# Gate and up projections of a streaming encoder layer by one level of Strassen's products

## Chip, core and metric

The kernel runs on one core of one Trainium2 chip. The metric is the device time of one execution in microseconds (us), median of three runs.

## What is computed

One layer of a hybrid encoder for 1024 prompt tokens and 32 sample tokens, width 1024: a combined projection, sparse attention, retention, a gated merge, and at the end the part that the change touches:

```
x1 = layer_norm(ALPHA * x + merged @ w_o, ln1_g, ln1_b)
h = jax.nn.silu(x1 @ w_gate) * (x1 @ w_up)          # w_gate, w_up: 1024 x 2816
return layer_norm(ALPHA * x1 + h @ w_down, ln2_g, ln2_b)   # w_down: 2816 x 1024
```

All inputs and outputs are float32.

## The kernel before

TensorE works on pairs of rounded numbers: every operand is split into a high part (`hi`, written as type `fp32r` by ScalarE) and a remainder (`lo = x - hi`, by VectorE or GpSimd), and each product is made of three matmuls, hi·hi, hi·lo and lo·hi, accumulated in PSUM (`tform` and `natural`, whose matmuls are all recorded by `chain`, L163). `split` (L139, L143) makes a pair; `unit` loads a 128x1024 weight tile into `raw` (two buffers), and splits it into `whi`, `wlo` (four buffers in `ring1`).

The tokens are 1056 columns: nine tiles of 128 (the last, tile 8, holds the 32 sample tokens), in three chunks of 384, 384 and 288 columns. A program on the host, `Weave`, sets the order of TensorE's instructions; the other engines' instructions are put in order by a scheduler, and each engine then works through its own in that order.

The end of the layer has two stages. `o_jobs` multiplies by w_o, tile by tile, in two halves of 512 columns. In the second half a layer norm follows each tile, and `x1_tile` transposes the result on TensorE (L988) and splits it into x1, eight tiles of 128 rows. `f_jobs` then goes through the 22 blocks of 128 hidden columns: for each chunk, 24 matmuls for gate (8 tiles of k, three products each), SiLU on ScalarE (L1085), 24 matmuls for up, a multiplication on VectorE out of PSUM (L1087), and the split of the result into `hh`, `hl`. After each second block, `down` adds the previous pair's part of h @ w_down: per token tile two outputs of 512 columns, 6 matmuls each, which VectorE adds to `yn` (L1058). The last call takes two pairs at once and ends each tile with the second layer norm.

PSUM has two banks under the name `g` and six under `m`; `f_jobs` uses the `m` ones.

Of the kernel before, what the change touches and what calls it, by code (L numbers as in the profile page):

```python
# [21 lines left out]
FB = 22  # L22
ALPHA = 2.0 ** 0.25
# [72 lines left out]
def body(ctx, tc, nc, a):  # L96
# [120 lines left out]
    mt_d = [dp.tile([D, n], F32, name=f"mtd{j}") for j, (_, n) in enumerate(CHUNKS)]  # L217
    r_d, r32_d = scratch(1, [8, 1152], "rd")[0], scratch(1, [8, 32, 1152], "r32")[0]
# [18 lines left out]
    def mbank():  # L237
        return psum.tile([128, 512], F32, name="m", bufs=6)
# [741 lines left out]
    def x1_tile(t, t_ln):  # L980
        c0, n = SEGS[t]
        j, o0 = chunk_of(t)
        yield 0.0, t_ln
        for q in range(2):
            pt = mbank()
            for i in range(4):
                k = q * 4 + i
                nc.tensor.transpose(pt[:, i * n:(i + 1) * n], yn[t][0:n, k * 128:(k + 1) * 128], ident[0:n, 0:n])  # L988
            split(x1[j][0][:, q * 4:(q + 1) * 4, o0:o0 + n], x1[j][1][:, q * 4:(q + 1) * 4, o0:o0 + n],
                  pt[:, 0:4 * n].rearrange("p (k c) -> p k c", k=4), "act", "dve")  # L990
# [40 lines left out]
    mtp.close()  # L1031
    ringE = Open("ringE", bufs=2, side="right")
    hp = Open("hid", side="right")
    g2 = hp.tile([128, D], F32, name="g2")
    b2 = hp.tile([128, D], F32, name="b2")
    dma(g2, bcast(a["ln2_g"], D))
    dma(b2, bcast(a["ln2_b"], D))

    def down(pairs, final):
        us = [u for pr in pairs for u in pr[0]]  # L1040
        for t in (8, *range(8)) if final else range(9):
            c0, n = SEGS[t]
            for hf in range(2):
                kk = [(u[0][:, hf * 512:(hf + 1) * 512], u[1][:, hf * 512:(hf + 1) * 512]) for u in us]
                o = mbank()
                if t < 8:
                    yield from natural(o, kk, lambda k: (pairs[k // 2][1][:, k % 2, c0:c0 + n],
                                                         pairs[k // 2][2][:, k % 2, c0:c0 + n]), 512)
                    src = o
                else:  # L1050
                    yield from natural_s(o, kk, lambda k: pairs[k // 2][3][:, k % 2, :], 512, hp)
                    src = merge_s(o, 512, hp)
                y = yn[t][0:n, hf * 512:(hf + 1) * 512]
                if final:
# [7 lines left out]
    def f_jobs():  # L1062
        def load(f):
            return blk(unit(a["w_gate"][f], ring1)), blk(unit(a["w_up"][f], ring1))

        prev = None
        nxt = load(0)
        for f in range(FB):
            i = f % 2
            if i == 0:  # L1070
                hh = hp.tile([128, 2, TT], F32R, name="hh", bufs=2)
                hl = hp.tile([128, 2, TT], F32R, name="hl", bufs=2)
                hs = hp.tile([128, 2, 64], F32R, name="hs", bufs=2)
            wg, wu = nxt
            if f + 1 < FB:
                nxt = load(f + 1)
            else:
                wl = [unit(a["w_down"][f - 1 + z], ring1) for z in range(2)]
            for j, (c0, n) in enumerate(CHUNKS):
                def rx(k):  # L1080
                    return x1[j][0][:, k, :], x1[j][1][:, k, :]
                pg, pu = mbank(), mbank()
                yield from tform(pg, wg, KT, rx, n)
                sg = hp.tile([128, 384], F32, name="sg", bufs=2)
                nc.scalar.activation(sg[:, :n], pg[:, :n], AF.Silu)  # L1085
                yield from tform(pu, wu, KT, rx, n)
                nc.vector.tensor_tensor(sg[:, :n], pu[:, :n], sg[:, :n], op=ALU.mult)  # L1087
                split(hh[:, i, c0:c0 + n], hl[:, i, c0:c0 + n], sg[:, :n], "act", "dve")
                if c0 + n == TT:
                    for jj, tl in enumerate((hh, hl)):  # L1090
                        nc.scalar.activation(hs[:, i, jj * 32:(jj + 1) * 32], f32(tl[:, i, T:TT]), AF.Copy)
            if i == 1:
                if f + 1 < FB:
                    if prev is not None:
                        yield from down([prev], False)
                    prev = ([unit(a["w_down"][f - 1 + z], ringE) for z in range(2)], hh, hl, hs)
        yield from down([prev, (wl, hh, hl, hs)], True)
# [128 lines left out]
```

## Time and profile before

| | |
|---|---|
| median of three runs (lowest to highest) | 1974.81 us (1972.91 to 1975.71) |
| the profiled execution | 1969.68 us, span 1967.6 us |
| TensorE matmul busy | 1918.1 us, 97% of the span |
| VectorE, ScalarE, GpSimd busy | 1141.0, 644.4, 654.2 us |
| gate, up and down stage | from about 1175 us of the span to its end |

Busy time of TensorE is a model of pipelined matmuls; how fast it goes is read from the distance between the starts of matmuls. A wait of another engine matters only where TensorE waits for that engine.

### The profile page before, as it was taken

What the parts mean: (1) busy time and instruction counts of PE and PEld (TensorE: products, weight loads), DVE (VectorE), ACT (ScalarE), POOL (GpSimd) and SP (SyncE); (2) the same over time, 40 slices, a digit from 0 to 9 for tenths busy, and PEclk for the clock granted to TensorE, in tenths of its full rate; (3) what the DMA queues carried; (4) which work ended last, traced back from release to release, by engine and by line L of the source; (5) the groups of instructions that cost most, each with busy time, mean ns of one, the idle gap of its engine ahead of it and who ended that gap; (6) DMA issues with size and microseconds to landing.
All of it is one profiled execution on the core that took longest, in us unless ns stands there. A gap on an engine that the chain in (4) does not pass through costs nothing. (4 is left out here: it accounts for less than half of the span.)

```text
span 1967.6 us, 28831 instructions
## 1 busy us (share of the span) xinstructions
PE 1918.1 (97%) x10785; PEld 1745.3 (89%) x10785; DVE 1141.0 (58%) x2335; ACT 644.4 (33%) x1352; POOL 654.2 (33%) x631
## 2 busy tenths in 40 slices
PE   8999999999999799999999999999999999999998
PEld 7899898787788799899999779998998998999896
DVE  4699889999981687876533483233333233324327
ACT  4553322423332555555422353121121121122122
POOL 4464443545454344442222233131132032032021
PEclk9999999999999899999999999999999999999999
DMA  5255642313217656534646532110110121011012
GB/s 182 86 171 202 223 134 80 94 50 92 57 53 190 176 151 163 149 113 138 222 131 198 163 105 79 40 65 16 50 65 33 33 65 44 22 65 54 12 42 89
DMA packets 138068, 201.40 MB, mean 102 GB/s; under 512 B 18992, under 2 KB 107048, under 8 KB 137928
## 3 DMA queue, kind: packets, MB, share of 16 engines
q1 hardware_dynamic: 131016, 190.90, 31.9%
q10 hardware_dynamic: 6912, 8.65, 1.3%
q8 instruction: 85, 1.39, 0.3%
q14 instruction: 55, 0.45, 0.1%
HBM read 149.06 MB, written 51.62 MB: 102 GB/s over the span
## 5 line engine op out<-in xcount | busy, mean ns | idle before, releaser
L143 POOL TENSOR_TENSOR wlo<-raw,whi 128x1024 fp32r<-128x1024 f32 (+1 forms) x132 | 319.3, 2424 | 820.8 <-ACT whi L139 770.3
L163 PE MATMUL m<-x,whi 128*128 128x384 f32 (+1 forms) x2112 | 504.4, 324 | 0.0
L163 PEld LDWEIGHTS m<-x,whi 128*128 128x128 f32 x2112 | 371.8, 189 | 1.4
L163 PE MATMUL m<-x,wlo 128*128 128x384 f32 (+1 forms) x1056 | 343.4, 325 | 0.0
L1087 DVE TENSOR_TENSOR sg<-m,sg 128x384 f32<-128x384 f32 (+1 forms) x66 | 34.6, 524 | 321.0 <-PE m L163 320.3
L139 ACT ACTIVATE whi<-raw 128x1024 fp32r<-128x1024 f32 x140 | 146.5, 1057 | 191.6 <-PE m L163 57.2
L163 PE MATMUL g<-xh,whi 128*128 128x384 f32 (+1 forms) x600 | 198.5, 331 | 0.5 <-ACT gev L673 0.5
L163 PE MATMUL g<-xh,wlo 128*128 128x384 f32 (+1 forms) x600 | 198.5, 331 | 0.2 <-POOL wlo L143 0.2
L163 PEld LDWEIGHTS m<-x,wlo 128*128 128x128 f32 x1056 | 198.5, 188 | 0.0
L163 PE MATMUL g<-xl,whi 128*128 128x384 f32 (+1 forms) x600 | 198.1, 330 | 0.0
L360 DVE MAX8 m<-sc 128x8 f32<-128x384 f32 (+6 forms) x209 | 182.3, 875 | 4.7
L361 DVE MATCH_REPLACE8 sc<-m,sc 128x384 f32<-128x384 f32 (+6 forms) x209 | 179.9, 861 | 0.2
L1058 DVE TENSOR_TENSOR yn<-m,yn 128x512 f32<-128x512 f32 x144 | 99.5, 691 | 94.6 <-PE m L163 94.6
L163 PE MATMUL m<-whi,hh 128*128 128x512 f32 x352 | 139.1, 395 | 0.0
L163 PE MATMUL m<-whi,hl 128*128 128x512 f32 x352 | 138.9, 395 | 0.0
L163 PE MATMUL m<-wlo,hh 128*128 128x512 f32 x352 | 138.5, 393 | 0.0
L744 POOL TENSOR_TENSOR P<-TB,mask 128x128 f32<-128x128 f32 (+8 forms) x72 | 92.7, 1304 | 126.2 <-PE m L806 98.1
L163 PEld LDWEIGHTS g<-xh,whi 128*128 128x128 f32 x600 | 113.4, 189 | 3.6 <-ACT gev L673 0.8
L163 PEld LDWEIGHTS g<-xl,whi 128*128 128x128 f32 x600 | 113.4, 189 | 2.8 <-issue 1.1
L163 PEld LDWEIGHTS g<-xh,wlo 128*128 128x128 f32 x600 | 113.7, 189 | 2.4 <-POOL wlo L143 0.5
L143 DVE TENSOR_TENSOR hl<-sg,hh 128x384 fp32r<-128x384 f32 (+1 forms) x66 | 75.6, 1146 | 53.0 <-ACT hh L139 53.0
L163 PE MATMUL g<-whi,xl 128*128 128x512 f32 x256 | 105.4, 412 | 0.0
(243 smaller groups left out, 3866.5 us busy)
## 6 DMA issues: line engine op xcount, KB each, us to landing
raw<-wT SPq DMA_DIRECT2D x34, 512.0 KB, 3.7
raw<-w_gate SPq DMA_DIRECT2D x22, 512.0 KB, 3.2
raw<-w_up SPq DMA_DIRECT2D x22, 512.0 KB, 3.2
raw<-w_down SPq DMA_DIRECT2D x22, 512.0 KB, 3.3
raw<-wr SPq DMA_DIRECT2D x16, 512.0 KB, 3.9
ml<-mtd SPq DMA_DIRECT2D x16, 512.0 KB, 5.8
KS<-kh SPq DMA_DIRECT2D x16, 392.0 KB, 6.4
KL<-kl SPq DMA_DIRECT2D x16, 392.0 KB, 9.1
```

Of the source, the lines that this page charges most:

```text
L139: nc.scalar.activation(hi, src, AF.Copy)
L143: e.tensor_tensor(lo, src, f32(hi), op=ALU.subtract)
L163: nc.tensor.matmul(out, lhsT=l, rhs=r, start=i == 0, stop=i == m - 1)
L360: nc.vector.max(m8[0:n], v)
L361: nc.vector.match_replace(v, m8[0:n], v, TAKEN)
L744: nc.gpsimd.tensor_tensor(pp[0:n, :Wd], TB[0:n, b0:b0 + Wd], masks[t][0:n, :], op=ALU.add)
L1058: nc.vector.tensor_tensor(y, src, y, op=ALU.add)
L1087: nc.vector.tensor_tensor(sg[:, :n], pu[:, :n], sg[:, :n], op=ALU.mult)
```

## The change

Blocks 0 and 1 are computed as before, but in column pieces of 264 (`u_plain`). For the other 20, x1 is kept as four quadrants (two halves of k by two halves of the columns; tile t goes to the half t mod 2, and each half holds 16 of the sample columns twice, so it is 528 wide), and two neighbouring blocks of a weight matrix with their two halves of k are the four quadrants of the other factor. Seven products replace the eight of the plain multiplication (`products`): sums of quadrants of x1 (`sums`: T1, T2, T3 and T4) are made once, T4 in the place of x1's quadrant B12, and sums of the quadrants of the weights for each pair of blocks and matrix (`Quad`) on GpSimd. Each product is 12 matmuls of 264 columns (4 tiles of k, three products), done for both pieces u = 0, 1 of the columns. `products` accumulates further products onto a bank whose earlier content was read out, so some products come after a read-out (`e1`, `u2`, `u3`). h goes to DRAM (`hd_d`), as does the scaled x1 (`x1_d`); `d_jobs` reads h back and does all of down afterwards. In the second half of `o_jobs` tile 8 comes first.

```diff
+HALF, SUB = 528, 264
...
+def place(t):
+    return t % 2, t // 4 * SUB + t // 2 % 2 * 128
...
+    hd_d, x1_d = scratch(FB, [128, 1024], "hd"), scratch(1, [TT, D], "x1d")[0]
...
-    x1 = [[fp.tile([128, KT, n], F32R, name=f"x1{i}_{j}") for i in range(2)] for j, (_, n) in enumerate(CHUNKS)]
+    x1 = [[[fp.tile([128, 4, HALF], F32R, name=f"x1{i}_{q}{h}") for i in range(2)] for h in range(2)] for q in range(2)]
...
     def x1_tile(t, t_ln):
...
+        dma(x1_d[c0:c0 + n, :], yn[t][0:n, :])
...
     def o_jobs():
...
-            for t in range(9):
+            for t in range(9) if hf == 0 else (8, *range(8)):
...
+    def went():
+        i = n_went[0] % 6
+        n_went[0] += 1
+        if i < 4:
+            return [ring1.tile([128, 1024], F32R, name=nm) for nm in ("whi", "wlo")]
+        return [mtp.tile([128, 8, 128], F32R, name=nm).rearrange("p a b -> p (a b)") for nm in ("mh", "ml")]
...
+    def sums(tp, t4):
...
+            whole(a_, B11)
+            whole(b_, B12)
+            nc.vector.tensor_tensor(a_, b_, a_, op=ALU.subtract)
+            whole(c_, B22)
+            nc.vector.tensor_tensor(b_, c_, b_, op=ALU.subtract)
+            nc.vector.tensor_tensor(c_, c_, a_, op=ALU.subtract)
+            cut(tq[2], c_)
+            cut(tq[3], b_)
+            cut(tq[1], a_)
+            whole(b_, B21)
+            nc.vector.tensor_tensor(c_, b_, c_, op=ALU.subtract)
...
+    def u_plain():
+        ws = [(went_of(a["w_gate"][f]), went_of(a["w_up"][f])) for f in range(2)]
+        sg = hg.tile([128, 2, TT], F32, name="sg", bufs=2)
+        while len(W.sides) > 2:
+            yield 0.2
+        for u in range(2):
+            if u == 1:
+                while W.sides:
+                    yield 0.2
+                ynp.close()
+                st["tset"] = Open("tset")
+                for z in range(1, 4):
+                    tq[z] = [st["tset"].tile([128, 4, HALF], F32R, name=f"T{z}{i}") for i in range(2)]
+                tp = Open("tsum", side="right")
+                t4 = tp.tile([128, 4, HALF], F32, name="t4")
+                sums(tp, t4)
+            s = slice(u * SUB, (u + 1) * SUB)
+            for f in range(2):
+                wg, wu = (blk(w) for w in ws[f])
+                for h in range(2):
+                    d = sg[:, f, h * HALF + u * SUB:h * HALF + (u + 1) * SUB]
+
+                    def rx(k):
+                        b = x1[k // 4][h]
+                        return b[0][:, k % 4, s], b[1][:, k % 4, s]
+                    pg, pu = mbank(), mbank()
+                    yield from tform(pg, wg, KT, rx, SUB)
+                    nc.scalar.activation(d, pg[:, :SUB], AF.Silu)
+                    yield from tform(pu, wu, KT, rx, SUB)
+                    nc.vector.tensor_tensor(d, pu[:, :SUB], d, op=ALU.mult)
+        for i in range(4):
+            split(T4[0][:, i, :], T4[1][:, i, :], t4[:, i, :], "act", "dve")
+        store_h(sg, 0)
+        tp.close()
+
+    class Quad:
+        def __init__(self, src, fp_):
+            self.r = [load_raw(src[2 * fp_ + i]) for i in range(2)]
+            a11, a12, a21, a22 = (r[:, z * 512:(z + 1) * 512] for r in self.r for z in range(2))
+            self.s1, self.s2 = (up.tile([128, 512], F32, name=f"qs{z}") for z in range(2))
+            P = nc.gpsimd.tensor_tensor
+            P(self.s1, a21, a22, op=ALU.add)
+            P(self.s2, self.s1, a11, op=ALU.subtract)
+            P(a21, a11, a21, op=ALU.subtract)
+            self.e = [went(), went()]
+            self.put(0, a11, self.s2)
+            self.put(1, a21, self.s1)
+
+        def put(self, i, *srcs):
+            for z, src in enumerate(srcs):
+                c = slice(z * 512, (z + 1) * 512)
+                split(self.e[i][0][:, c], self.e[i][1][:, c], src, "act", "dve")
+
+        def more(self):
+            a12, a22 = (r[:, 512:1024] for r in self.r)
+            self.e.append(went())
+            self.put(2, a12, a22)
+            nc.gpsimd.tensor_tensor(a12, a12, self.s2, op=ALU.subtract)
+
+        def last(self):
+            self.e.append(went())
+            self.put(3, self.r[0][:, 512:1024])
+
+    def products(q, u, sg, gate, hooks, order=range(7)):
+        s = slice(u * SUB, (u + 1) * SUB)
+        pa, pb, pc, pd = gbank(), mbank(), mbank(), mbank()
+        e1, u2, u3 = (up.tile([128, SUB], F32, name=nm, bufs=2) for nm in ("e1", "u2", "u3"))
+        d = [[sg[:, f, h * HALF + u * SUB:h * HALF + (u + 1) * SUB] for h in range(2)] for f in range(2)]
+        add, mul = ALU.add, ALU.mult
+        V, P = nc.vector.tensor_tensor, nc.gpsimd.tensor_tensor
+        todo = ((pa, 0, 0, B11), (pb, 0, 1, tq[2]), (pd, 1, 0, tq[3]), (pc, 1, 1, tq[1]),
+                (pa, 2, 0, B21), (pd, 2, 1, T4), (pc, 3, 0, B22))
+        for z in order:
+            bank, i, c, b = todo[z]
+            w = half_of(q.e[i], c)
+            o = bank[:, :SUB]
+            for k in range(4):
+                for j, (l, r) in enumerate(((0, 0), (0, 1), (1, 0))):
+                    nc.tensor.matmul(o, lhsT=w[l][:, k, :], rhs=b[r][:, k, s], start=z < 4 and k == 0 and j == 0,
+                                     stop=k == 3 and j == 2, skip_group_check=True)
+                    yield mm(SUB)
+            if z == 0:
+                nc.scalar.activation(e1, o, AF.Copy)
+            elif z == 1:
+                V(u2, o, e1, op=add)
+            elif z == 2:
+                V(u3, o, u2, op=add)
+            elif z == 3:
+                V(d[1][1] if gate else u3, o, u3, op=add)
+            elif z == 4:
+                if gate:
+                    nc.scalar.activation(d[0][0], o, AF.Silu)
+                else:
+                    V(d[0][0], o, d[0][0], op=mul)
+            elif z == 5:
+                V(d[1][0] if gate else e1, o, u2, op=add)
+            else:
+                V(d[0][1] if gate else u2, o, u2, op=add)
+            if z in hooks:
+                hooks[z]()
+        for (f, h), t in (((1, 1), u3), ((1, 0), e1), ((0, 1), u2)):
+            if gate:
+                nc.scalar.activation(d[f][h], d[f][h], AF.Silu)
+            else:
+                P(d[f][h], d[f][h], t, op=mul)
...
+    def u_jobs():
...
+        for x, (m, f) in enumerate(seq):
+            q = nxt
+            if m == 0:
+                sg = hg.tile([128, 2, TT], F32, name="sg", bufs=2)
+            if x + 1 < len(seq):
+                nxt = make(*seq[x + 1])
+                hooks = {1: nxt.more, 3: nxt.last}
+            else:
+                first.append(went_of(a["w_down"][0]))
+                first.append(went_of(hd_d[0], "dve"))
+                hooks = {1: lambda: first.append(went_of(a["w_down"][1])),
+                         3: lambda: first.append(went_of(hd_d[1], "dve"))}
+            if x == 0:
+                g = [products(q, u, sg, True, hooks if u else {}, (0, 4, 1, 2, 3, 5, 6)) for u in range(2)]
+                for z in range(2):
+                    for _ in range(24):
+                        yield next(g[z])
+                yield from g[0]
+                yield from g[1]
+            else:
+                yield from products(q, 0, sg, m == 0, {})
+                yield from products(q, 1, sg, m == 0, hooks)
+            if m == 1:
+                store_h(sg, 2 * f)
...
+    def d_jobs():
+        cur = ([0, 1], [first[0], first[2]], [first[1], first[3]])
+        for i in range(FB // 2):
...
+                for z in range(2):
+                    us[z] = went_of(a["w_down"][fs[z]])
+                    hh[z] = h_of(fs[z])
...
+            yield from down(*cur, "first" if i == 0 else "mid")
...
-    def f_jobs():
...
-                if f + 1 < FB:
-                    if prev is not None:
-                        yield from down([prev], False)
...
```

Three places show how the instructions stand. The first is ScalarE where the plain pair ends and the first products begin. Before, the first block of `f_jobs` looks so (`sg<-m` SiLU, `x_2<-m` and `yn` the sample tile's x1, `hh<-sg` and `whi<-raw` splits):

```order
L1085 ACTIVATE sg<-m 128x384
L139 ACTIVATE x_2_12383<-m 128x4x32 x2
L993 ACTIVATE yn_12378<-yn_12378 32x1024
L139 ACTIVATE hh<-sg 128x384
L1085 ACTIVATE sg<-m 128x384
L139 ACTIVATE hh<-sg 128x384
L139 ACTIVATE whi<-raw 128x1024
```

Now, with what each waits for (`x_01<-t` is the high part of T4, `e<-g` the read-out of the first product for u = 0 and, lower, for u = 1; `qs` are the GpSimd sums, `mh<-raw` and `whi<-raw` splits of weight quadrants):

```order
L148 ACTIVATE x_01_12394<-t_13496 128x528 [waits PE_49] x3
L148 ACTIVATE x_01_12394<-t_13496 128x528 [waits DVE_49,PE_49]
L1191 ACTIVATE e_13845<-g 128x264 [waits DVE_49,PE_49]
L1200 ACTIVATE sg<-g 128x264 [waits PE_49]
L148 ACTIVATE mh<-raw 128x512 [waits Pool_49]
L148 ACTIVATE whi<-raw 128x512 [waits Pool_49]
L1191 ACTIVATE e_13877<-g 128x264 [waits PE_49]
```

A read-out that TensorE needs now stands behind a wait for VectorE, and a second one behind splits that wait for GpSimd. The second place is VectorE and GpSimd at the same spot: the end of the sums and the first splits of weights on VectorE, then the four sums of the first weights on GpSimd.

```order
L152 TENSOR_TENSOR x_01_12395<-t_13496,x_01_12394 128x528 x2
L1138 TENSOR_TENSOR sg<-m,sg 128x264
L152 TENSOR_TENSOR T_13490<-t_13496,T_13489 128x528
L152 TENSOR_TENSOR hs<-sg,hs 128x32
L1107 TENSOR_TENSOR t_13496<-ts_13546,t_13496 128x528
L152 TENSOR_TENSOR x_01_12395<-t_13496,x_01_12394 128x528
L152 TENSOR_TENSOR ml<-qs_13791,mh 128x512
```

```order
L1150 TENSOR_TENSOR qs_13791<-raw 128x512
L1151 TENSOR_TENSOR qs_13792<-qs_13791,raw 128x512
L1152 TENSOR_TENSOR raw<-raw 128x512
L1166 TENSOR_TENSOR raw<-raw,qs_13792 128x512
```

Before, GpSimd had only `wlo<-raw,whi 128x1024` and the small layer-norm steps here. The buffers `qs`, `e1`, `u2` and `u3` lie where `t4` and `ts` lay, so the first of them wait for the last read of `t4`. The third place is VectorE in the stage itself. Before, a block was three times

```order
L1087 TENSOR_TENSOR sg<-m,sg 128x384
L143 TENSOR_TENSOR hl<-sg,hh 128x384
```

and now, from the second piece of a gate product into the next up product (`u<-m,e` and the like read products out of PSUM, `wlo<-...` split the weights of the pair after):

```order
L1193 TENSOR_TENSOR u_14422<-m,e_14421 128x264
L152 TENSOR_TENSOR wlo<-raw,whi 128x512 x2
L1195 TENSOR_TENSOR u_14423<-m,u_14422 128x264
L1197 TENSOR_TENSOR sg<-m,u_14423 128x264
L152 TENSOR_TENSOR wlo<-raw,whi 128x512
L1204 TENSOR_TENSOR sg<-m,u_14422 128x264
L152 TENSOR_TENSOR wlo<-raw,whi 128x512
L1206 TENSOR_TENSOR sg<-m,u_14422 128x264
L152 TENSOR_TENSOR wlo<-qs_14533,whi 128x512
L1193 TENSOR_TENSOR u_14555<-m,e_14554 128x264
L152 TENSOR_TENSOR wlo<-qs_14534,whi 128x512
L1195 TENSOR_TENSOR u_14556<-m,u_14555 128x264
```

The splits of the next weights now stand between the read-outs on which later products wait.

## Rows read from the trace of the kernel before

**Rows 1.** The page's first lines: busy time, share of the span and instructions of each engine.

```profile
span 1967.6 us, 28831 instructions
PE 1918.1 (97%) x10785; PEld 1745.3 (89%) x10785; DVE 1141.0 (58%) x2335; ACT 644.4 (33%) x1352; POOL 654.2 (33%) x631
```

**Rows 2.** What TensorE waited for from 1100 us to the end: line waited for, total us, times, longest us. These are all.

```profile
PE m L988 <- issue: 2.3, 1, 2.3
PE m L988 <- DVE yn L967: 1.8, 1, 1.8
```

**Rows 3.** The chain of work that ended last, in order of time: start us, us, what. A pair of blocks with its down is 288 + 96 matmuls of L163 and some of L183 to L189; the last stretch of 288 is gate and up of the last pair alone.

```profile
1439.96 68.90 PE m L163 x384
1508.87 0.23 PE m L183
...
1510.70 68.90 PE m L163 x384
...
1864.40 46.62 PE m L163 x288
```

**Rows 4.** TensorE in order of time: start us, us, shape. Two starts of chunks of 384 columns, 63 matmuls apart; two of 288, 27 matmuls apart; pairs of 256 and of 128 columns in the attention.

```profile
1300.26 0.34 PE L163 MATMUL m<-x,wlo 128*128 128x384 f32 x1
...
1311.39 0.34 PE L163 MATMUL m<-x,wlo 128*128 128x384 f32 x1
...
1200.17 0.30 PE L163 MATMUL m<-x,wlo 128*128 128x288 f32 x1
...
1203.74 0.29 PE L163 MATMUL m<-x,wlo 128*128 128x288 f32 x1
...
802.46 0.28 PE L831 MATMUL m<-pl,V 128*128 128x256 f32 x1
802.58 0.27 PE L806 MATMUL m<-ident,P 128*128 128x128 f32 x1
...
803.04 0.22 PE L753 MATMUL m<-KS,QS 128*128 128x128 f32 x1
803.10 0.28 PE L755 MATMUL m<-KL,QS 128*128 128x128 f32 x1
```

**Rows 5.** The stage by 200 us: busy us of each engine (instructions), granted clock, DMA share, GB/s; and the weight loads, GpSimd's and ScalarE's splits of the weights in 1200 to 1900 us: busy us, mean ns, idle before.

```profile
1300.00:1500.00 200.00, 200.00 (x1123) 187.18 (x1122) 66.61 (x87) 38.32 (x70) 44.39 (x18) 1.00 0.15 48
...
L163 PEld LDWEIGHTS m<-x,whi 128*128 128x128 f32 x1989 | 349.2, 188 | 1.2
...
L143 POOL TENSOR_TENSOR wlo<-raw,whi 128x1024 fp32r<-128x1024 f32 x62 | 154.7, 2500 | 549.8 <-ACT whi L139 549.8
...
L139 ACT ACTIVATE whi<-raw 128x1024 fp32r<-128x1024 f32 x62 | 64.6, 1056 | 80.0 <-PE m L163 26.4 <-DMA raw<-w_gate 18.4 <-issue 18.1
...
L139 ACT ACTIVATE x<-m 128x512 fp32r<-128x512 f32 x12 | 6.6, 590 | 3.8 <-PE m L988 3.8
...
L1085 ACT ACTIVATE sg<-m 128x288 f32<-128x288 f32 x22 | 8.8, 401 | 20.5 <-PE m L163 20.5
```

**Rows 6.** VectorE's operations: duration ns least/median/most. `hl` reads two operands in SBUF, `sg<-m` and `yn<-m` read one in PSUM.

```profile
L143 DVE TENSOR_TENSOR hl<-sg,hh x66: 457/559/2449, 1191.6 to 1912.1; 128x384 fp32r<-128x384 f32 x44, 128x288 fp32r<-128x288 f32 x22
...
L1087 DVE TENSOR_TENSOR sg<-m,sg x66: 456/557/559, 1189.9 to 1911.1; 128x384 f32<-128x384 f32 x44, 128x288 f32<-128x288 f32 x22
...
L1058 DVE TENSOR_TENSOR yn<-m,yn x144: 683/692/693, 1275.8 to 1862.6; 128x512 f32<-128x512 f32 x144
```

**Rows 7.** VectorE and GpSimd between 1248 and 1255 us: start us, us, shape [idle before, releaser].

```profile
1251.16 0.46 DVE L1087 TENSOR_TENSOR sg<-m,sg 128x288 f32<-128x288 f32 x1 [4.64 <-PE m L163]
1252.43 2.43 DVE L143 TENSOR_TENSOR hl<-sg,hh 128x288 fp32r<-128x288 f32 x1 [0.81 <-ACT hh L139]
...
1248.97 2.40 POOL L143 TENSOR_TENSOR wlo<-raw,whi 128x1024 fp32r<-128x1024 f32 x1 [17.79 <-ACT whi L139]
1252.14 2.40 POOL L143 TENSOR_TENSOR wlo<-raw,whi 128x1024 fp32r<-128x1024 f32 x1 [0.77 <-ACT whi L139]
```

**Rows 8.** Stretches of 2 us around TensorE's two waits of rows 2: columns as in rows 5 (TensorE's busy time is the first, the granted clock the third from the end).

```profile
1134.00:1136.00 2.00, 0.00 (x1) 0.00 (x0) 2.00 (x2) 0.00 (x0) 0.00 (x0) 1.00 1.03 388
...
1186.00:1188.00 2.00, 0.41 (x3) 0.09 (x1) 1.29 (x3) 0.81 (x1) 0.65 (x2) 1.00 0.00 0
1188.00:1190.00 2.00, 1.70 (x13) 1.58 (x14) 1.32 (x4) 1.88 (x4) 0.00 (x0) 1.00 0.40 129
1190.00:1192.00 2.00, 2.00 (x9) 2.00 (x8) 1.28 (x4) 1.56 (x4) 0.00 (x0) 0.50 1.00 295
1192.00:1194.00 2.00, 2.00 (x9) 2.00 (x8) 0.16 (x1) 0.12 (x1) 0.00 (x0) 0.64 0.27 104
```

**Rows 9.** The transposes of the sample tile's x1, the last of the nine, on TensorE, in order of time.

```profile
1188.19 0.94 PE L988 MATMUL m<-ident,yn 32*128 32x32 f32 x8 [1.77 <-DVE yn L967]
```

**Rows 10.** Weight loads from DRAM: issues, KB each, median us from issue to landing.

```profile
raw<-w_gate SPq DMA_DIRECT2D x22, 512.0 KB, 3.2
```

More of the change, by code (lines that the diff above doesn't have):

```diff
@@ L981, in x1_tile @@
         c0, n = SEGS[t]
-        j, o0 = chunk_of(t)
         yield 0.0, t_ln
@@ L1030, in body @@
     ringD.close()
-    mtp.close()
-    ringE = Open("ringE", bufs=2, side="right")
-    hp = Open("hid", side="right")
+    hsp = Open("hsp", side="right")
+    hs = hsp.tile([128, FB, 64], F32R, name="hs")
+    hg = Open("hgate", side="right")
+    B11, B12, B21, B22 = x1[0][0], x1[0][1], x1[1][0], x1[1][1]
+    T4 = B12
+    tq = {}
+    n_went = [0]
+    def went():
[4 more added lines that the diff above has]
+        return [mtp.tile([128, 8, 128], F32R, name=nm).rearrange("p a b -> p (a b)") for nm in ("mh", "ml")]
@@ new lines, in sums, with whole, cut @@
+    def sums(tp, t4):
+        for k in range(4):
+            a_, b_ = (tp.tile([128, HALF], F32, name=f"ts{z}") for z in range(2))
+            c_ = t4[:, k, :]
+            def whole(out, b):
+                nc.vector.tensor_tensor(out, f32(b[0][:, k, :]), f32(b[1][:, k, :]), op=ALU.add)
+            def cut(t, src):
+                split(t[0][:, k, :], t[1][:, k, :], src, "act", "dve")
+            whole(a_, B11)
[9 more added lines that the diff above has]
+            nc.vector.tensor_tensor(c_, b_, c_, op=ALU.subtract)
@@ new lines, in body @@
+    first = []
+    def u_jobs():
+        seq = [(m, f) for f in range(1, FB // 2) for m in range(2)]
+        make = lambda m, f: Quad(a["w_gate" if m == 0 else "w_up"], f)
+        nxt = make(*seq[0])
+        nxt.more()
+        nxt.last()
+        for x, (m, f) in enumerate(seq):
[17 more added lines that the diff above has]
+                yield from g[1]
+            else:
+                yield from products(q, 0, sg, m == 0, {})
+                yield from products(q, 1, sg, m == 0, hooks)
+            if m == 1:
+                store_h(sg, 2 * f)
@@ L1034, in body @@
+    W.main(u_plain())
+    up = Open("up", side="right")
+    W.main(u_jobs())
+    up.close()
+    hg.close()
+    st["tset"].close()
+    fp.close()
+    ynp = Open("yn2")
+    sm = ynp.tile([128, 9, 2], F32, name="sm")
+    yn = [ynp.tile([128, D], F32, name=f"yo{t}") for t in range(9)]
+    hp = Open("hid")
     g2 = hp.tile([128, D], F32, name="g2")
     b2 = hp.tile([128, D], F32, name="b2")
[L1036 to L1040, printed above, removed]
+    ringE = Open("ringE", bufs=6, side="right")
@@ L1041, in down, with h_of @@
+    def h_of(f):
+        r = load_raw(hd_d[f])
+        e = [ringE.tile([128, 1024], F32R, name=nm) for nm in ("hhi", "hlo")]
+        split(e[0], e[1], r, "act", "dve")
+        return e
+    def down(fs, us, hh, kind):
+        final = kind == "final"
         for t in (8, *range(8)) if final else range(9):
```

110 lines of the change are left out of this document (66 added, 44 removed).

## The prediction

> **What bounds the kernel now.** I read the busy table first [rows 1]: TensorE 97%, the next engine 58%. A modelled busy time alone proves little, so next the waits: from 1100 us on TensorE waits twice, 2.3 and 1.8 us, both around the layer norm [rows 2]. Third the chain [rows 3]: from 1439.96 to 1510.70 us it stays on TensorE, a pair of blocks with its down in 70.74 us, and gate and up of a pair alone (288 matmuls) take 46.62 us. Fourth the pace inside [rows 4]: 63 matmuls of 384 columns in 11.13 us, 0.177 us each; 27 of 288 in 3.57 us, 0.132 us each. Both are 0.46 ns per column, at a granted clock of 1.00 [rows 5]. So the stage costs TensorE's columns and nothing else, and VectorE (66.61 of 200 us), ScalarE and GpSimd have room [rows 5]. Fewer columns give time, as long as nobody is late with an operand.
>
> **Products.** Before, a pair has 192 matmuls of 384 and 96 of 288 columns: 46.62 us / 288 / 352 columns = 0.460 ns per column [rows 3]. Now a pair has 2 matrices x 2 pieces x 7 products x 12 = 336 matmuls of 264 columns. At 0.460 ns that is 0.1214 us each and 40.80 us; 10 pairs give 58.2 us less. The plain pair has as many columns as before and costs nothing new. Is there a floor for short matmuls with a weight load each? A load is recorded with 188 ns [rows 5], yet at 288 columns loads follow every 132 ns, and in the attention a matmul of 256 columns took 0.12 us and one of 128 columns 0.06 us [rows 4]: no floor down there. Bounds: at the pace of 288 columns, 0.132 us, all 3744 matmuls of 264 (384 plain, 3360 in products) take 494 us against 22 x 23.31 = 513, a gain of only 19; the 0.12 us of 256 columns scaled is 0.124 us and 464 us, a gain of 49. I take 58, since two shapes agree on 0.460.
> The Trainium skill (TensorE: Matmul & The Clock Gate, Back-to-back issue gap) says that in a stream of load and matmul pairs both set the spacing, and gives a warm gap of N/2.4 + 2.5 ns; by that gap the products would gain an estimated 51 us. The trace has 177 ns where it gives 162.5, and agrees on no fixed cost that matters [rows 4].
>
> **Down as a stage.** The matmuls are the same, 70.74 - 46.62 = 24.1 us a pair. VectorE now also splits h there: 16 additions of 0.69, the sample tile's some 3.2 and two subtractions of 1.2 us (twice 128x512) make 17 us of 24.1 [rows 6]; six banks cover 8 us of lateness. The loads (four of 3.2 us a pair [rows 10]) have a whole pair's time. Cost: nothing; without this cover it would be a load and a split, some 5 us, once.
>
> **The sample tile earlier.** Its transposes waited 1.8 us for its layer norm [rows 9] and then the granted clock was 0.50 and 0.64 for 4 us, which costs 1.7 us [rows 8]. Now over 40 matmuls of other tiles lie between. Gain 3.5 us; 0 if another tile's norm is late instead.
>
> **The turn into the products.** Here I expect new waits. Let E be the end of the plain pair on TensorE, 46.6 + 2.1 us of transposes after its start. VectorE: two-operand work takes 0.457 us at 288 and 0.559 at 384 columns [rows 6], so 0.71 at 528, 0.69 at 512 and 0.43 at 264. `sums` and what its order mixes in are, after tile 7's transposes (14.5 us into the pair), 47 operations of 0.71 and 12 smaller ones, 39 us: done near 54 us, E + 5.6. Even an idle VectorE could not end before E + 4.8, since T4 overwrites B12, which the plain pair reads until E - 1.5. ScalarE's order puts the first `e1` behind T4's last part, and `e1` lies in `t4`'s memory. TensorE's order is product 0 and then product 4 in the same bank, which must wait for `e1`: TensorE does 1.46 us (12 matmuls), then waits to E + 6.0. GpSimd's four sums (1.2 us each, half of 2.4 [rows 7]) start only then too. The `e1` of u = 1 stands on ScalarE behind the split of the fourth: R + 4.8 + 0.3 of hand-overs + 0.55 + 0.4 = R + 6.1 with R = E + 5.6; product 4 of u = 1 ends at E + 13.2. These 48 matmuls would have ended at E + 5.8: 7.4 us lost (6.6 with an idle VectorE, some 20 more if its operations met GpSimd each time, at `hl`'s worst [rows 6]). After a wait of 2.3 us the clock stayed up, after 1.8 us it fell for 4 us [rows 8], so I add 1.7 us once (0 to 3.4). Next late: VectorE's read-out `u2` stands behind a split that needs the next weights, whose load waits for `raw` to be free: 3.2 us [rows 10], ScalarE, VectorE, so product 5 starts some 1 us late.
>
> **The pairs after that.** A weight matrix of a pair takes 20.4 us on TensorE. VectorE has 7 splits of 0.69 and 10 or 12 read-outs of 0.43 us, 9 to 10.5 us; GpSimd 4.8, with up 8.6; ScalarE 8. Loads fit; the order is the risk. `raw` is free when the last split of the coming weights is done, about 17.3 us into a matrix; the two loads land at 20.5 and, if they share the queue, near 22; then GpSimd sums twice, ScalarE and VectorE split, and behind this split stands the read-out (`u3`) on which product 5 waits. I get it at 5.5 us of the next matrix; product 5 needs it at 7.3. The slack is near 1.8 us, and GpSimd and VectorE take some of it: a subtraction that started 0.3 us after a GpSimd operation took 2.43 us instead of 0.46, while the read-out from PSUM was not held [rows 7]. I take 0.2 us of waiting per matrix, 4 us; from 0 to 4.8 us each, if all four sums hold VectorE in full.
>
> **Sum.** -58.2 - 3.5 + 7.4 + 1.7 + 1.0 + 4.0 = -47.6: span 1967.6 to 1920.0. The profiled execution was 1969.68 us, the median of the runs 1974.81, 0.26% above it; I carry both: 1922 for an execution with a profile, **1927 us** for the median.
>
> **Rivals.**
> (a) Forecast, 1918 to 1936: chance 0.60.
> (b) The weights come late in each matrix by 0.7 to 1.5 us, when the two loads land one after the other, 3.2 us apart: 10 to 26 us more, 1937 to 1953. For it: the chain has six steps and two queues in fixed order; against: all loads are light here, DMA share 0.15 [rows 5]. Chance 0.19.
> (c) Slower than before: the same chain, and each GpSimd sum also waits out a VectorE subtraction and holds the next: three times 0.69 on top, 2.8 us per matrix, 56 us, so 1979. It turns the sign from 2.6 us per matrix on. For it: both durations of rows 7 show whole operations waiting; against: the read-outs are not held, and VectorE and GpSimd together have 14 of 20.4 us with both operands in SBUF. Chance 0.06.
> The Trainium skill (SBUF — State Buffer, "SBUF: two separate sides") says that GpSimd and a VectorE operation with two SBUF inputs take this port exclusively, the loser waiting for the whole instruction; the trace agrees, 2.43 us [rows 7].
> (d) Short matmuls have a floor of 0.132 us: gain 19, 1967. Against it the 0.12 and 0.06 us [rows 4]. Chance 0.04.
> (e) The turn costs little and nothing waits after: 1911 to 1918. Chance 0.11.
>
> **How the numbers follow.** 0.2%, 4 us, is about what a measurement of this kernel can tell from no change. (a), (b) and (e) are faster by more, and half of (d): 0.92; between lie rest of (d) and a little of (c): 0.03; slower 0.05. The range from 1911 to 1950 takes in (a), (e) and most of (b), and with them the bounds of 49 us for the products, of the clock and of the turn; it leaves out (c), (d) and the tail of (b).
>
> **What would show it.** Right: 264-column matmuls 0.121 us apart and a matrix in 20.4 us; TensorE's waits at the turn on ScalarE's `e` (L1191), near 4.5 and 2.8 us; down pairs of 24.1 us; VectorE around half busy. Wrong: product 5 or 6 (waiting on VectorE, L1195 or L1197) late in every matrix; GpSimd's sums longer than 1.2 us; a pace of 0.13 us or more; a granted clock under 1.0 within the products; a wait at the start of down or in its first pairs for h.

## The result and the profile after

The changed kernel takes **1928.97 us** (median of 4 runs, 1926.99 to 1930.08), the kernel before 1973.86 us in the same comparison: a ratio of 0.977, 95% interval 0.976 to 0.979. The forecast was 1927, within 1911 to 1950. The profiled execution took 1926.99 us, its span is 1925.0 against 1967.6.

First the page's span and the row of its busy table, as [rows 1] of before. VectorE's share rose from 58 to 67%.

```profile
span 1925.0 us, 30894 instructions
...
PE 1865.7 (97%) x11361; PEld 1690.9 (88%) x11361; DVE 1297.6 (67%) x2647; ACT 712.9 (37%) x1484; POOL 740.6 (38%) x740
```

Second, TensorE's waits from 1100 us on (what waited, for whom: us in total, times, longest), as [rows 2]. The two waits around the layer norm are replaced by one of 5.0 us on `mh`, and the turn into the products brings the two on `e`:

```profile
PE m L192 <- DVE mh L152: 5.0, 1, 5.0
PE g L1187 <- ACT e L1191: 4.8, 2, 3.0
PE m L172 <- DVE yo L1293: 1.1, 2, 0.8
PE m L1187 <- DVE u L1195: 0.8, 2, 0.5
PE m L998 <- DVE yn L978: 0.4, 1, 0.4
```

Third, the chain, as [rows 3]. A product takes 12 matmuls; the `g` rows shown are product 0 of three pieces in a row. From the first to the third it is as much as a whole matrix: 1620.48 to 1640.88 us, 20.40 us for 168 matmuls, 0.1214 us each. The pair of down shown here takes 24.25 us (24.0 on average over five), and from 1716 us to the last tile TensorE leads the chain (from 1644 to 1716 us it runs through loads and splits of w_down and h, but TensorE's own waits in down are 1.1 us in all):

```profile
1620.48 1.47 PE g L1187 x12
...
1630.71 1.45 PE g L1187 x12
...
1640.88 1.46 PE g L1187 x12
...
1724.21 22.40 PE m L172 x96
...
1748.46 21.80 PE m L172 x96
```

To see where the time went I cut both executions at the same places on TensorE: the first matmul of the output projection, the end of the plain pair (before: of the first pair; called E), the first matmul of down, the end.

| stretch, us | before | after | difference |
|---|---|---|---|
| up to the output projection's first matmul | 1070.9 | 1072.8 | +1.9 |
| from there to E | 156.7 | 158.3 | +1.6 |
| the other ten pairs of gate and up | 466.2 | 419.8 | -46.4 |
| down | 273.8 | 274.1 | +0.3 |
| span | 1967.6 | 1925.0 | -42.6 |

(Before, pairs and down alternate, so 466.2 is ten times the 46.62 of [rows 3] and down the rest.) The first line is no effect of the change: in the kernels below, which are alike up to there, it lies between 1070.9 and 1075.5 us in the profiled executions. In the third line 3360 matmuls of 0.1214 us are 407.9 us, 58.3 less than before; the remaining 11.9 us are losses: 8.4 at the turn (the first 48 matmuls end at 1244.47, 13.3 us after E = 1231.15, and would take 5.8; then the clock is low for 0.9 us more) and 3.5 spread over the later gate matrices.

### The profile page after: what moved, and what is told of

It reads as the page before. It is cut to its first block, busy times and chain, and to the rows that moved or that the text cites. A ratio compares the mean times of both kernels' runs of the same rounds, so it can differ in the third digit from the quotient of the medians.

```text
span 1925.0 us, 30894 instructions
## 1 busy us (share of the span) xinstructions
PE 1865.7 (97%) x11361; PEld 1690.9 (88%) x11361; DVE 1297.6 (67%) x2647; ACT 712.9 (37%) x1484; POOL 740.6 (38%) x740
## 5 line engine op out<-in xcount | busy, mean ns | idle before, releaser
L152 POOL TENSOR_TENSOR wlo<-raw,whi 128x1024 fp32r<-128x1024 f32 (+1 forms) x84 | 199.3, 2376 | 352.5 <-ACT whi L148 296.1
L148 ACT ACTIVATE whi<-raw 128x1024 fp32r<-128x1024 f32 (+1 forms) x159 | 138.5, 883 | 204.1 <-PE m L172 34.3
L1293 DVE TENSOR_TENSOR yo<-m,yo 128x512 f32<-128x512 f32 x128 | 85.4, 686 | 43.6 <-PE m L172 42.0
L1187 PE MATMUL m<-T,whi 128*128 128x264 f32 x624 | 114.6, 283 | 0.0
L172 PE MATMUL g<-whi,xh 128*128 128x512 f32 x256 | 104.9, 410 | 0.0
L172 PE MATMUL g<-wlo,xh 128*128 128x512 f32 x256 | 104.2, 407 | 0.0
L1187 PEld LDWEIGHTS m<-T,whi 128*128 128x128 f32 x624 | 96.7, 188 | 0.0
L172 PE MATMUL m<-rT,whi 128*128 128x384 f32 (+1 forms) x384 | 91.2, 323 | 0.4 <-DVE rT L152 0.4
L1187 PE MATMUL m<-T,wlo 128*128 128x264 f32 x312 | 88.6, 284 | 0.0
L172 PE MATMUL m<-xh,whi 128*128 128x384 f32 (+1 forms) x240 | 80.4, 335 | 5.5 <-ACT xh L148 5.5
```

Source lines behind the costliest of these rows:

```text
L148: nc.scalar.activation(hi, src, AF.Copy)
L152: e.tensor_tensor(lo, src, f32(hi), op=ALU.subtract)
L172: nc.tensor.matmul(out, lhsT=l, rhs=r, start=i == 0, stop=i == m - 1)
L1187: nc.tensor.matmul(o, lhsT=w[l][:, k, :], rhs=b[r][:, k, s], start=z < 4 and k == 0 and j == 0, stop=k == 3 and j == 2, skip_group_check=True)
L1293: nc.vector.tensor_tensor(y, src, y, op=ALU.add)
```

## Experiments

The table gives each kernel by the same stretches of its profiled execution, the median of its runs and the ratio to before.

| kernel | to E | ten pairs | down | median us | ratio, 95% interval |
|---|---|---|---|---|---|
| changed | 158.3 | 419.8 | 274.1 | 1928.97 | 0.977 (0.976 to 0.979) |
| all_plain | 158.3 | 466.0 | 273.9 | 1973.77 | 1.0005 (0.9995 to 1.0014) |
| turn_apart | 158.3 | 413.1 | 275.6 | 1919.77 | 0.973 (0.972 to 0.975) |
| e1_apart | 158.5 | 418.4 | 274.5 | 1925.49 | 0.977 (0.975 to 0.978) |
| lo_gpsimd | 158.4 | 417.1 | 275.9 | 1925.87 | 0.977 (0.975 to 0.978) |
| sum_twice | 158.4 | 417.6 | 274.7 | 1925.08 | 0.976 (0.975 to 0.977) |
| sum_five | 158.8 | 425.8 | 273.6 | 1935.16 | 0.982 (0.980 to 0.983) |
| tile8_ring | 157.9 | 421.0 | 275.4 | 1928.26 | 0.978 (0.976 to 0.979) |
| tile8_late_norm | 156.0 | 419.2 | 275.0 | 1925.33 | 0.975 (0.974 to 0.977) |
| tile8_second | 153.6 | 418.9 | 274.5 | 1922.96 | 0.974 (0.973 to 0.976) |
| all_three | 155.5 | 409.1 | 273.6 | 1913.75 | 0.970 (0.968 to 0.971) |
| best | 153.8 | 409.1 | 275.6 | 1913.08 | 0.970 (0.969 to 0.972) |

Down varies by 2 us between kernels that are alike there, so no difference of that size is read from a span; the stretches say more.

**Is it the products?** `all_plain` replaces the product matrices by the plain loop:

```diff
-    W.main(u_jobs())
+    W.main(u_rest())      # pairs 1 to 10: for f, u, h: tform(gate), tform(up), 264 columns
```

> The change without Strassen: all 22 blocks are computed plainly, in pieces of 264 columns, and everything else is as in the changed kernel (h through DRAM, down as a stage of its own, the sample tile first). Theory A, the whole gain is the products' fewer columns, and down as a stage costs and gives nothing: the 46.4 us that the product stage saved come back, span 1969 to 1975, near before's 1967.6. Theory B, part of the gain lies in the new down stage or in the shorter pieces: span below 1960. Theory C, the new stage costs something that the products hide: span above 1980.

The ten pairs take 466.0 us again, down 273.9, and the time is that of before. Theory A holds: splitting into pieces of 264 columns, h through DRAM and down as its own stage gain nothing and cost nothing; all of the gain is in the products.

**The turn.** `turn_apart` keeps the first matrix's intermediate tiles out of the memory of `t4`:

```diff
+        sg0 = hg.tile([128, 2, TT], F32, name="sg", bufs=2)
+        nxt = Quad(a["w_gate"], 1, (sg0[:, 1, 0:512], sg0[:, 0, HALF:HALF + 512]))   # s1, s2
+        if len(order) == 7 and order[1] == 4:
+            e1, u2, u3 = d[1][1], d[0][1], d[1][1]
```

> The changed kernel, with the first product matrix's e1, u2, u3 and GpSimd's two sums kept in the second sg buffer, which is free then, and not in t4's memory. Theory A, it is t4's memory that makes TensorE wait at the turn: the two waits on e1 (3.0 and 1.8 us) and the half clock behind them (some 3.6 us) go, 7 to 8.4 us, span near 1917. Theory B, VectorE and GpSimd are what is late at the turn: the four sums now run while VectorE builds the T operands, each holds one of its operations up by a microsecond, and TensorE waits for T instead; the span falls by less than 3 us.

In the changed kernel the turn looks like this (start us, us, engine, line, tiles; idle time before in brackets): the last low part of T4 on VectorE, GpSimd's first sum, then `e1` on ScalarE and the matmul that waited for it.

```profile
1228.79 1.71 ACT L148 ACTIVATE x<-t 128x528 fp32r<-128x528 f32 x3
...
1233.83 0.64 ACT L148 ACTIVATE x<-t 128x528 fp32r<-128x528 f32 x1 [1.19 <-DVE t L1107]
1235.30 0.39 ACT L1191 ACTIVATE e<-g 128x264 f32<-128x264 f32 x1 [0.83 <-DVE x L152]
...
1241.32 0.63 ACT L148 ACTIVATE whi<-raw 128x512 fp32r<-128x512 f32 x1 [1.05 <-POOL raw L1166]
1241.85 0.37 ACT L1191 ACTIVATE e<-g 128x264 f32<-128x264 f32 x1
```

```profile
1234.50 0.71 DVE L152 TENSOR_TENSOR x<-t,x 128x528 fp32r<-128x528 f32 x1 [0.77 <-ACT x L148]
1237.25 2.91 DVE L152 TENSOR_TENSOR ml<-qs,mh 128x512 fp32r<-128x512 f32 x2 [2.04 <-ACT mh L148]
```

```profile
1235.29 1.27 POOL L1150 TENSOR_TENSOR qs<-raw 128x512 f32<-128x512 f32 x1 [45.76 <-DVE x L152]
...
1239.57 1.72 POOL L1166 TENSOR_TENSOR raw<-raw,qs 128x512 f32<-128x512 f32 x1
```

```profile
1235.74 0.50 PE L1187 MATMUL g<-x,whi 128*128 128x264 f32 x2 [2.99 <-ACT e L1191]
...
1242.28 0.51 PE L1187 MATMUL g<-x,whi 128*128 128x264 f32 x2 [1.82 <-ACT e L1191]
```

ScalarE's `e1` and GpSimd's first sum both start within 0.1 us of 1235.21, when T4 is done. The second `e1` stands behind the split of the fourth sum (1239.57 and 1.72 us later). With the tiles apart, two waits of 0.5 us are left (waits of `turn_apart`), and the ten pairs take 6.7 us less. Theory A holds; 7 to 8.4 was slightly too much.

```profile
PE g L1190 <- ACT sg L1194: 1.0, 2, 0.5
```

`e1_apart` makes the second of the two edits only:

> The changed kernel, with only e1, u2 and u3 of the first product matrix in the free sg buffer; GpSimd's two sums stay in t4's memory. Theory A, both stand behind T4: the 48 matmuls of products 0 and 4 run through to 5.8 us after the plain pair's end, then product 1 waits for the split of s2, which ended 9.0 us after it in the changed kernel: one wait of 3.1 us and some 1.7 us of half clock in place of 8.4 us, span near 1921.5. Theory B, e1 alone makes the turn's wait: no wait is left, as with both apart, span 1918.

Only 1.4 us come back. Products 0 and 4 run through, then product 1 waits 1.0 and 0.4 us, shorter than the 3.1 expected, but the next matrix's sums and read-outs are late too: two further waits of 1.2 and 0.9 us in the same matrix, on read-outs. So neither theory's number holds: GpSimd's sums still stand behind T4, as A said, and what is late there travels on through VectorE's and GpSimd's order. Waits of `e1_apart`:

```profile
PE m L1190 <- DVE sg L1198: 1.2, 1, 1.2
PE m L1190 <- ACT mh L148: 1.0, 1, 1.0
PE g L1190 <- ACT sg L1194: 1.0, 2, 0.5
PE m L1190 <- DVE sg L1200: 0.9, 1, 0.9
```

**The later matrices.** In each gate matrix from the second on, product 5 of the first piece starts 0.25 to 0.77 us late, 3.6 us in nine; in the up matrices it doesn't. One of them, VectorE, GpSimd and the matmul that waited (same columns):

```profile
1363.35 0.17 DVE L152 TENSOR_TENSOR hs<-sg,hs 128x32 fp32r<-128x32 f32 x1
1365.58 1.82 DVE L152 TENSOR_TENSOR wlo<-qs,whi 128x512 fp32r<-128x512 f32 x1 [2.05 <-ACT whi L148]
1367.32 1.27 DVE L152 TENSOR_TENSOR hs<-sg,hs 128x32 fp32r<-128x32 f32 x1
1368.52 0.42 DVE L1193 TENSOR_TENSOR u<-m,e 128x264 f32<-128x264 f32 x1
1368.86 0.68 DVE L152 TENSOR_TENSOR wlo<-qs,whi 128x512 fp32r<-128x512 f32 x1
1369.46 0.42 DVE L1195 TENSOR_TENSOR u<-m,u 128x264 f32<-128x264 f32 x1
```

```profile
1365.56 1.29 POOL L1151 TENSOR_TENSOR qs<-qs,raw 128x512 f32<-128x512 f32 x1
1366.81 1.74 POOL L1152 TENSOR_TENSOR raw<-raw 128x512 f32<-128x512 f32 x1
```

```profile
1369.93 0.51 PE L1187 MATMUL m<-x,whi 128*128 128x264 f32 x2
```

The split of 32 sample columns (`hs`) took 0.17 us at 1363.35 and 1.27 us at 1367.32, where it ended together with GpSimd's sum; behind it stand the read-outs `u2` (L1193) and `u3` (L1195), and product 5 started 0.05 us after `u3`. A split of 0.69 us took 1.82. The `hs` splits (32 sample columns, 8 in each piece of 264, so 16 in each half) follow an up matrix and so fall into the next gate matrix alone. In all nine late gate matrices `u3` ends 7.3 to 7.9 us after the matrix's start, where product 5 could start at 7.3; in the up matrices it ends at 7.0 us or before. Three kernels test what that means; the first has the `lo` lines alone, the other two the last line alone.

```diff
-            self.put(0, a11, self.s2)
-            self.put(1, a21, self.s1)
+            self.put(0, a11, self.s2, lo="pool")      # lo_gpsimd
+            self.put(1, a21, self.s1, lo="pool")
+            P(self.s1, a21, a22, op=ALU.add)          # sum_twice: once more; sum_five: four times more
```

> The changed kernel, with the four low parts of a11, s2, a21 and s1 of each product matrix but the first subtracted on GpSimd and not on VectorE. In the changed kernel product 5 of each gate matrix's first piece starts 0.25 to 0.77 us late (3.6 us in ten matrices). Theory A, it is late because VectorE's read-out u3 stands behind these splits, which wait for the weights: the 3.6 us go, span near 1921.5. Theory B, VectorE is held by GpSimd through operands in SBUF, and more work on GpSimd holds it longer or makes the weights late: the time is the same or up to 10 us longer.

> The changed kernel, with GpSimd's first sum of each product matrix made twice (1.28 us more in the chain from the landed weights to the splits). Theory A, this chain has no slack left in gate matrices and 0.24 us in up matrices, since product 5 waits for a read-out behind it: 9 x 1.28 + 9 x 1.04 + 1.3 at the turn, some 22 us, span near 1947. Theory B, the chain has room and the small losses are something else: under 5 us, span below 1930.

> The changed kernel, with GpSimd's first sum of each product matrix made five times (5.1 us more in the chain, after twice cost nothing). Theory A, the chain of the weights has room for it, because a12, a22 and the fourth sum wait for TensorE's later products anyway, and what made product 5 late was only how many splits stand ahead of the read-out u3 on VectorE: span within 4 us of 1925. Theory B, the room ends between 1.3 and 5.1 us: the weights come late in each matrix by up to 3.8 us, span up to 1995.

In `lo_gpsimd` the late starts are gone from all nine gate matrices, though an `hs` split still takes 1.0 us in each, and a new wait of 0.8 us near the turn leaves a gain of 2.6 us: theory A. In `sum_twice` they are gone too but for one of 0.3 us, although the chain is 1.28 us longer: theory A missed by 22 us there. The scheduler that lays out VectorE's work had put it in another order for the longer sum, with the read-outs further ahead, so this kernel doesn't show what a longer chain costs at the order of the changed kernel; the same matrix in `sum_twice`:

```profile
1365.06 1.00 DVE L152 TENSOR_TENSOR hs<-sg,hs 128x32 fp32r<-128x32 f32 x1 [2.51 <-ACT hs L148]
1365.99 0.42 DVE L1194 TENSOR_TENSOR u<-m,e 128x264 f32<-128x264 f32 x1
1366.71 1.22 DVE L152 TENSOR_TENSOR wlo<-qs,whi 128x512 fp32r<-128x512 f32 x1 [0.31 <-ACT whi L148]
1367.86 0.42 DVE L1196 TENSOR_TENSOR u<-m,u 128x264 f32<-128x264 f32 x1
1368.20 1.44 DVE L152 TENSOR_TENSOR wlo<-qs,whi 128x512 fp32r<-128x512 f32 x1
```

Both `hs` splits and one weight split stand ahead of `u3`, not two, and it ends 0.5 us before product 5 (1368.80). `sum_five` lengthens the chain further, again with an order of its own. Its ten pairs take 6.0 us more: it loses 3.4 more in the first matrix and some 6 more in the next four, while from then on no product is late at all (the changed kernel lost some 3 us there). Its waits on `e` and on read-outs, and VectorE in a later gate matrix, whose product 5 starts at 1463.64:

```profile
PE g L1191 <- ACT e L1195: 3.5, 2, 3.0
PE m L1191 <- DVE u L1199: 3.4, 3, 2.6
```

```profile
1459.82 0.99 DVE L152 TENSOR_TENSOR hs<-sg,hs 128x32 fp32r<-128x32 f32 x1 [2.44 <-ACT hs L148]
1460.73 0.42 DVE L1197 TENSOR_TENSOR u<-m,e 128x264 f32<-128x264 f32 x1
1461.26 0.43 DVE L1199 TENSOR_TENSOR u<-m,u 128x264 f32<-128x264 f32 x1
```

From the sixth matrix on no split of GpSimd's sums (`wlo<-qs`) stands ahead of `u3`, which here ends 1.95 us before product 5. The wait of 2.6 us lies in the fourth matrix, where `u3` (1329.87 us) stands behind four splits of weights. GpSimd is busy for 229 us between 1300 and 1640 us, where it was 133 in the changed kernel (columns: sum of busy time on TensorE, its loads, VectorE, ScalarE, GpSimd; granted clock, DMA share, GB/s):

```profile
1300.00:1640.00 340.00, 338.75 (x2777) 337.07 (x2776) 182.56 (x312) 109.37 (x229) 132.96 (x115) 1.00 0.24 79
```

My expectation of a span within 4 us of 1925 missed (1933.8, of which 2.7 lie before the output projection). Theory A holds for the later matrices alone: with no such split ahead of `u3`, 5.1 us more in the chain cost a steady matrix nothing. Where such splits stand ahead of it, as in the changed kernel, what is late in the chain reaches product 5.

**The sample tile.** [Rows 2, 9] had waits of 2.3 and 1.8 us. After, TensorE stands 5.0 us at 1121 and then works at a granted clock of 0.50 for 4 us (first three windows, columns as above; the fourth is the rest of the output projection, the last two belong to the turn):

```profile
1121.00:1126.00 5.00, 0.22 (x1) 0.00 (x0) 2.98 (x3) 2.46 (x4) 3.14 (x2) 0.76 0.35 110
1126.00:1128.00 2.00, 1.79 (x5) 0.88 (x6) 0.76 (x3) 0.55 (x1) 1.37 (x1) 0.50 0.19 38
1128.00:1130.00 2.00, 2.00 (x6) 0.94 (x5) 0.00 (x0) 0.00 (x0) 0.99 (x1) 0.50 1.10 351
1132.00:1182.65 50.65, 50.25 (x250) 41.39 (x248) 40.83 (x62) 29.66 (x47) 16.97 (x17) 1.00 0.49 159
1236.00:1238.00 2.00, 2.00 (x12) 2.00 (x12) 0.75 (x1) 0.68 (x2) 1.92 (x3) 0.56 0.00 0
1244.00:1246.00 2.00, 2.00 (x11) 2.00 (x10) 0.04 (x1) 1.02 (x2) 0.00 (x0) 0.50 0.88 315
```

The loads of the merged heads take turns on three buffers, two of `mtp` and one of `op`, by the tile's number; the sample tile gets the `op` buffer in both halves. Since it is now last in one half and first in the next, its load waits for its own predecessor's matmuls. Three kernels:

```diff
-        p = mtp if (9 * hf + t) % 3 < 2 else op
+        p = mtp if (9 * hf + (t + 1) % 9 if hf else t) % 3 < 2 else op      # tile8_ring
-                    W.spawn(x1_tile(t, layer_norm(op, t, sm[:, t, :], g1, b1) + 2.0))
+                    W.spawn(x1_tile(t, layer_norm(...) + (7.0 if t == 8 else 2.0)))   # tile8_late_norm: both
-            for t in range(9) if hf == 0 else (8, *range(8)):
+            for t in range(9) if hf == 0 else (0, 8, *range(1, 8)):      # tile8_second: this alone
```

> The changed kernel, with one thing different: the loads of the merged heads take their buffers in the order in which the output projection uses them, so that the second half's first tile (the sample tile) no longer gets the one buffer that the first half's last tile still holds. Theory A, the buffer makes TensorE wait: in the changed kernel TensorE stands 5.0 us for this tile's split and then runs some 10 matmuls at half pace (2 us); both go, a new wait of up to 1 us for the tile's norm may come, so the span falls by 6 to 7 us, from 1925.0 to 1918 or 1919. Theory B, the load would be late with any buffer, because it stands in the queue behind the loads of weights and x: the 5.0 us stay and the time is the same.

> The kernel with buffers in order of use (tile8_ring), and the transposes of the sample tile put 5 us later into TensorE's order. There TensorE stood 4.0 us for this tile's norm. Theory A, the tile was late only against the place that the order gave its transposes: with 5 us of other matmuls ahead of them the wait and the half clock behind it go, 151 to 152.5 us from the first matmul of the output projection to the end of the plain pair (157.9 with the wait), span 1919 or 1920. Theory B, the wait moves to the next tile's transposes or to the plain pair's start: 156 us or more, span 1924 or more.

> The changed kernel, with the sample tile second and not first in the second half of the output projection, so that its buffer has 5.6 us to come free and its norm is not the first. From the first matmul of the output projection to the end of the plain pair the changed kernel takes 158.3 us, some 151 of them without waits. Theory A, the first tile of the second half always waits, by the buffer or by its norm, and the sample tile waits only because it is first: tile 0 now waits some 2.3 us for its norm, as before the change, and the sample tile not at all: 153 to 154 us, span 1920 or 1921. Theory B, the sample tile's own longer chain (merge and norm) costs 4 us wherever it stands: 157 us, span 1924.

`tile8_ring` shows that the buffer was the cause of the 5.0 us, which are gone, but the gain isn't there: the transposes now stand 4.0 us for the tile's norm. `tile8_late_norm` went theory B's way, 156.0 us: TensorE waits 2.4 us for the next tile's norm and 1.4 for a split of x1 (presumably for the bank that it frees) instead. `tile8_second` gives 153.6, as theory A said, though with waits of 1.6, 0.5 and 0.4 us elsewhere and not 2.3 for tile 0's norm. Waits of the three, in that order:

```profile
PE m L998 <- DVE yn L978: 4.0, 1, 4.0
```

```profile
PE m L998 <- DVE yn L978: 2.4, 1, 2.4
...
PE m L998 <- DVE x L152: 1.4, 1, 1.4
```

```profile
PE m L998 <- DVE x L152: 1.6, 1, 1.6
...
PE m L172 <- DVE ml L152: 0.5, 1, 0.5
```

Why the waits move on there I didn't test. VectorE, busy for 40.8 of 50.7 us in the fourth window above (ScalarE 29.7, GpSimd 17.0), has the least room of the engines that feed TensorE, which fits.

**Together.** `all_three` joins `tile8_late_norm`, `turn_apart` and `lo_gpsimd`; `best` has `tile8_second` in place of the first.

> The changed kernel with the three edits together: buffers in order of use and the sample tile's transposes later, the first product matrix apart from t4's memory, and the four low parts on GpSimd. Theory A, the three losses stand apart and add: 6.7 us at the turn, 3.6 in the steady matrices and some 6.5 at the sample tile off 1925.0, a span of 1906 to 1911. Theory B, they share their cause (the order of VectorE), and one edit's gain comes back as another's wait: 1914 to 1918, no better than the turn alone.

> The changed kernel with the sample tile second, the first product matrix apart from t4's memory, and the four low parts on GpSimd. By the stretches of the runs so far: 153.6 us to the plain pair's end (sample tile second), 409.1 for the products (all three edits), 273.6 to 275 for down: 1.5 to 2 us less than the three edits with the sample tile first, span 1908 to 1910.

`all_three` has a span of 1910.9, just inside theory A; the sample tile gave 2.8 us of the 6.5 that A counted on. Products take 409.1 us, 1.2 over TensorE's own 407.9, so the turn and the steady matrices are nearly cleared. `best` is the same within its interval (span 1911.3; the first stretch came out at 153.8 and the products at 409.1 as forecast, but down took 275.6), and so misses the forecast of 1908 to 1910. It beats the changed kernel by 16 us and the kernel before by 3.0% (2.8 to 3.1). Its largest waits left are 2.0 us in down, 1.5 us for a split of x1 and 1.0 us at the turn.

## Why the prediction was right, step by step

- **Products, -58.2.** Right: 0.1214 us a matmul and 20.40 us a matrix, -58.3; `all_plain` confirms that nothing else gains. Rival (d) is out. By the gap that the Trainium skill gives for an isolated matmul (TensorE: Matmul & The Clock Gate, Back-to-back issue gap) it would have been an estimated 51; the trace has 0.121, 0.132 and 0.177 us for 264, 288 and 384 columns and goes by columns alone.
- **Down, 0.** Right: +0.3 us, 24.25 us a pair, waits of 1.1 us in its start.
- **The sample tile, -3.5.** Wrong: +1.6. The step looked only at the transposes, which indeed waited just 0.4 us. It did not ask what else of that tile moves: its load, and the buffer that it shares with its own namesake of the first half. Waits of 2.3 and 1.8 us and 1.7 us of low clock went, waits of 5.0 and 0.4 us and some 2 us of low clock came. This term alone was 5.1 us off, the largest error.
- **The turn, +7.4 and +1.7 for the clock.** The sum was right (13.3 us from E to the end of the 48 matmuls, forecast 13.2; 8.4 us in all against 9.1), its parts were not. The waits were 3.0 and 1.8 us, not 4.5 and 2.8, since T4 was done at E + 4.1 and not E + 5.6. My floor of E + 4.8 was wrong: I took B12 as one tile to be overwritten, but its splits follow the plain pair row by row, and the first began at E - 2.4. GpSimd's four sums took 6.0 us and not 4.8 (1235.29 to 1241.29). The clock fell twice, not once, and cost some 3.1 us; 0.5 us more went with the restarts after the two waits. That these parts add up to the forecast sum is luck. That `e1` and the sums wait for `t4`'s memory was right (`turn_apart`).
- **Product 5 at the turn, +1.0.** Not there: no such late start in the first two matrices.
- **The steady matrices, +4.0.** Right in size (3.5) and, for the order that this kernel has, in the step: `u3` stands behind splits of the coming weights, the first of which waits for ScalarE and GpSimd's first sum, and product 5 waits for `u3`. I had `u3` at 5.5 us of a matrix, 1.8 us before it is needed, with GpSimd and VectorE taking some of that slack. In the matrix shown they took 2.2 us, 1.1 on a split and 1.1 on `hs`; without them it would end at 5.1 us (an estimate from the durations shown). What the step lacked is the `hs` split, so that gate matrices alone are late, 0.4 us in nine and not 0.2 in twenty, and that the slack belongs to VectorE's order: with the splits elsewhere (`lo_gpsimd`, `sum_five`) the loss is gone. What GpSimd's hold alone costs at the old order no run shows. Rival (b), the weights late by 0.7 us or more in each matrix, didn't come: one start was that late. Rival (c) named a mechanism that is there: the Trainium skill (SBUF — State Buffer, "SBUF: two separate sides") says that a GpSimd operation that reads SBUF and a VectorE operation with two inputs in SBUF hold each other off for a whole instruction, and the trace agrees, 1.27 us for 0.17. It stayed cheap, because most of it fell into the slack and the read-outs from PSUM weren't held (0.42 or 0.43 us throughout).
- **The signs of being wrong.** Three of those I named showed in small: product 5 late (in nine matrices), GpSimd's sums longer than 1.2 us (1.27 to 1.76) and a granted clock under 1.0 in the first matrix. Of the signs of being right, VectorE is around half busy in the products, 183 of 340 us.
- **From the profiled execution to the median.** 1926.99 and 1928.97: 0.10% where 0.26 was carried. So the execution was missed by 5 us and the median by 2, and 3 us of that closeness are luck.

The sum came to -47.6 against -42.6: the sample tile's 5.1 us too little, 2.2 us too much over the turn and the steady matrices, and 1.9 us of chance ahead of it all.

## What to carry to other kernels

When an edit moves a tile to another place in the order, list everything the tile drags along (load, buffer slot, norm, transposes) and ask of each who held its buffer last: buffers that are dealt by number collide when the order changes. When a new stage opens in memory that the old one frees last, the first small tiles of the new stage inherit that wait; a buffer that is free anyway was worth 6.7 us here. And when a wait of a few tenths recurs, look at what stands ahead of the awaited operation in its engine's order before pricing the chain behind it: the slack of a chain holds for one order alone.

## What the runs showed of the hardware

The granted clock fell after the 3.0 us wait and after the 1.8 us wait that followed 4.7 us later: 0.56 and 0.50, the lower of its two levels of 1.2 and 2.4 GHz for most of these windows (the last two of those shown for the sample tile). It did not fall in `turn_apart`, where the two waits at the same places were 0.5 us.

The length of a wait alone doesn't decide it: in `sum_five` TensorE stood 3.0 us at the first of these places as well (the wait on `e`, until 1238.91), and the clock stayed at 1.00:

```profile
1239.00:1241.00 2.00, 2.00 (x17) 2.00 (x18) 0.00 (x0) 0.33 (x1) 1.92 (x2) 1.00 0.00 0
```

So 4.8 of the turn's 8.4 us were waits, and some 3.1 were the clock behind them (some 30 matmuls 0.22 us apart in place of 0.121). And I had not expected that a longer sum on one engine could make a stage faster: in `sum_twice` the ten pairs took 2.2 us less than in the changed kernel (417.6 against 419.8), with VectorE in another order. The spans differ by 3.2 us, but 1.7 of that lies ahead of the output projection, where the two kernels are alike.
